# The mixers' input projections in five groups of up to 512 columns, in place of nine of 256

## The chip, the cores and the metric

The kernel runs on one core of one Trainium2 chip. The metric is the device time of one execution in microseconds; lower is better. All times below are of that one core.

## What is computed

The reference is a small language model's forward pass on 256 tokens of width 1024: two layers of a first block, then one layer of another kind with a state-space part and sixteen experts. The change lies in the first block's mixers, of which there is one in each of its two layers:

```python
for l in range(DEPTH):                       # DEPTH = 2
    x = x + 0.5 * swiglu(rmsnorm(x, ffn1_norm[l]), ffn1_wg[l], ffn1_wu[l], ffn1_wd[l])
    h = rmsnorm(x, mix_norm[l]) @ w_in[l]                    # 256 x 1024 @ 1024 x 2290
    h_a, h_b, h_c = jnp.split(h, [A_COLS, A_COLS + B_COLS], axis=-1)
    o_a = mla_mixer(h_a, ...)    # low-rank q and kv, rope, 6 heads of causal attention
    o_b = nsa_mixer(h_b, ...)    # q and kc, vc, ks, vs, kw, vw, gates: compressed, selected, window
    o_c = diff_mixer(h_c, ...)   # q, k, v: 4 heads, the difference of two softmaxes
    x = x + jnp.concatenate([o_a, o_b, o_c], axis=-1) @ w_out[l]
    x = x + 0.5 * swiglu(rmsnorm(x, ffn2_norm[l]), ...)
```

In the second mixer, `kc` and `vc` are compressed: blocks of 32 tokens, 16 apart, plus a position vector, go through `silu(blk @ w1) @ w2`. The second part of the model is untouched by the change.

## The kernel before

Everything is kept in float32 and multiplied in pairs: a weight and an activation are each split into a high half (`h` in `wh`, `xhl`) that is rounded to the matmul's type and a low half (`wl`) with what is left, and a product is the sum of three matmuls, high by high, low by high, high by low. `load` (L145) brings eight chunks of 128 rows by 256 columns into one of four `st` buffers through SP's queue. `split` (L153) makes two `wh` and two `wl` of 1024 columns out of it, in rings of six; ScalarE writes `wh` (L166), VectorE subtracts for `wl` (L167). All matmuls go through `mm` (L97), so their line in the profile is L98, and groups are told apart by their tiles. Plain copies that scale go through a short helper, and stand at L524 in the profile.

A mixer (`_mixer`, L519) has eight banks of PSUM in four rings: `S` three, `T` two, `O` one, `W` two (L313). Its input projection `h` is made in nine groups (L533) of 242 or 256 columns, each for two tiles of 128 tokens, so that a bank `win` of 512 columns holds both. A group has 8 chunks x 2 token tiles x 3 = 48 products. ScalarE then copies its columns out, scaled by the token's inverse norm, into `hA`, `hQ`, `hV`, `hC` and `hW`: `hA` is what the first kind of heads needs, `hQ` and `hV` the second kind's, `hC` and `hW` the third's.

The string `ORDER` (L40) says in which order the steps of a mixer are written: `w` with digits is a group (`w01` two groups in turn), `mp`, `np`, `dp` prepare the three kinds of heads (L626, L770, L886), `m0`, `n0`, `d0` and so on are heads, `df` ends the third kind. A queue of fetches (L573 to L589) is made from the same string: four are issued at the start, and one more behind each group and behind `mp` and `np`. The first groups take the banks `W`, `W`, `S`, `S`, all others the ring `W` (L595).

The order in the text isn't yet the order on the engines. The whole program goes through a scheduler that simulates the engines and orders each one's instructions by its own costs, as far as data and buffers allow.

`np` is the step that matters below. It applies rope to `hQ` (`rtmp`, `hQ`), transposes the columns of `kc` and `vc` (`kvc`, L777, L778), copies them in four pieces to `Z` on ScalarE and VectorE in turn (L784), adds the position vectors (`blk`, L790, four pieces), and multiplies by `phi` (`h<-blk,phi`). The activation of `h` (ScalarE's L797, VectorE's L798) is followed by the small products `kcmp` and `vcmp`. `qtb` and `ktb` are transposes of the second kind's queries and keys; `ks` and `kw` are the keys' copies. `dp` applies rope to `hC`, transposes it (`qct` at L899, `kct` at L900) and copies the keys to `kC` (L905). Then come the scores `S`, the maxima `mx` (L725) and the softmax. At a mixer's end `wo` multiplies by `w_out` (loop at L972).

Of the kernel before, what the change touches and what calls it, by code (L numbers as in the profile page):

```python
# [22 lines left out]
KD = 8  # L23
# [16 lines left out]
ORDER = "w01 w5 w2 mp m0 m1 w8 w3 w4 w6 np w7 dp m2 m3 d0 d1 n0 n1 d2 d3 n2 n3 n4 n5 m4 df m5"  # L40


class Block:
# [128 lines left out]
    def cols(self, w, *segs):  # L172

        wv = w.rearrange("(k p) c -> p k c", p=128)
        out, c = [], 0
        for a, b in segs:
            out.append((c, wv[:, :, a:b]))
            c += b - a
        return self.load(out, wv.shape[1], c)
# [339 lines left out]
    def _mixer(self, l, xops, after):  # L519
# [6 lines left out]
        def tok(name, n, tag=None, bufs=1):  # L526
# [19 lines left out]
        def fetch(i):  # L546
            if i < len(groups):
                units[i] = self.cols(w_in, *groups[i][0])
# [26 lines left out]
        for step in steps:  # L575
            if step[0] == "w":
                for c in step[1:]:
                    queue.append(lambda i=int(c): units.update({i: self.cols(w_in, *groups[i][0])}))
# [18 lines left out]
        def w_in_groups(ids):  # L597

            ws = [self.split(units[i], "k") for i in ids]
            ps = [self.bank(tags.pop(0) if tags else "W", "win") for _ in ids]  # L600
            for k0 in range(KD):
                for k, i, t in ([(k0, i, t) for i in range(len(ids)) for t in range(2)] if len(ids) > 1 else
                                [(k, 0, k0) for k in range(KD)] if k0 < 2 else []):
                    w, p, n = ws[i], ps[i], units[ids[i]][2]
                    o = p[:, t * 256:t * 256 + n]
                    ts = slice(t * 128, (t + 1) * 128)
                    first = t == 0 and k == 0
                    last = t == 1 and k == KD - 1
                    wh, wl = (v[:, k % 4] for v in w[k // 4])
                    self.mm(o, xh[:, k, ts], wh, first, False)  # L610
                    self.mm(o, xh[:, k, ts], wl, False, False)
                    self.mm(o, xl[:, k, ts], wh, False, last)
            for i, p in zip(ids, ps):
                for dst, d, c, m in groups[i][1]:
                    for t in range(2):
                        src = p[:, t * 256 + c:t * 256 + c + m]
                        if isinstance(d, tuple):

                            o = dst[:, t, 0:384].rearrange("p (u c) -> p u c", c=64)[:, d[0] // 64::2][:, 0:d[1]]
                            src = src.rearrange("p (u c) -> p u c", c=64)  # L620
                        else:
                            o = dst[:, t, d:d + m]
                        ACT(o, src, scale=r[:, t:t + 1])
# [329 lines left out]
        for step in steps:  # L953
# [10 lines left out]
            elif step[0] == "w":  # L964
                w_in_groups([int(c) for c in step[1:]])
                for _ in step[1:]:
# [950 lines left out]
```

## Time and profile before

| what | value |
|---|---|
| time, median of three runs | 1533.76 us (1532.36 to 1533.86) |
| time of the profiled execution | 1532.0 us |
| its span in the profile | 1529.8 us |
| busy share of TensorE / VectorE / ScalarE / GpSimd | 98% / 67% / 48% / 6% |
| mixer of the first layer | about 201 to 340 us of the span |
| mixer of the second layer | about 714 to 853 us of the span |

The span runs from the first instruction to the last in the profile; the execution's own time has some 2 us around it. PE is TensorE, DVE VectorE, ACT ScalarE, POOL GpSimd and SP the engine that issues the loads. In a timeline the row of a matmul shows its duration with the pipeline's latency in it, so that what one costs is read from its start to the start of the next. A row that ends in x4 is four instructions in one. The bracket at a row's end is the engine's idle time ahead of it, and the instruction that ended it. The second mixer repeats the first some 512.8 us later.

### The profile page before, as it was taken

Reading aid. Unit: us, or ns where it says so; the run is one execution under the profiler, and the core shown is the slowest. Engines: PE = TensorE matmul, PEld = TensorE weight load, DVE = VectorE, ACT = ScalarE, POOL = GpSimd, SP = SyncE. Lnnn points to the kernel's source line nnn. Section 1 sums busy time; section 2 is a strip of 40 time slices with the busy share of each in tenths; the row PEclk is TensorE's granted clock in tenths of the full one; section 3 lists DMA queues with packets and bytes.
Section 4 is the critical chain, followed back from the end, with each engine's and each line's share of the span. In section 5 each row is a group of like instructions: output and inputs, shape, how many; then the busy total and the mean of one; then the engine's idle time right before and its main releaser. Section 6 shows DMA issues by size and latency. Waiting matters only on the chain.

```text
span 1529.8 us, 25415 instructions
## 1 busy us (share of the span) xinstructions
PE 1492.0 (98%) x9970; PEld 1253.6 (82%) x9970; DVE 1025.1 (67%) x2013; ACT 729.7 (48%) x1382; POOL 91.4 (6%) x142
## 2 busy tenths in 40 slices
PE   8999999999999999999999999999899999999996
PEld 7999998788999989999888999999799987344432
DVE  6886775868677786778576877779988875122112
ACT  6555565755454555455665655547554442011011
POOL 0000000520000000000025000000510100000000
PEclk9999999999999999999999999999999999999999
DMA  7756664216555565655640555566533588999993
GB/s 252 246 175 193 189 164 145 78 56 205 186 188 193 167 193 192 193 192 164 169 130 2 193 185 176 192 192 207 153 123 116 189 296 336 359 393 393 393 394 117
DMA packets 223559, 308.93 MB, mean 202 GB/s; under 512 B 20908, under 2 KB 167608, under 8 KB 223432
## 3 DMA queue, kind: packets, MB, share of 16 engines
q1 hardware_dynamic: 223128, 306.71, 60.1%
q8 instruction: 80, 1.31, 0.4%
q10 hardware_dynamic: 304, 0.53, 0.1%
q14 instruction: 47, 0.39, 0.1%
HBM read 306.16 MB, written 1.05 MB: 201 GB/s over the span
## 4 chain that ended last, share of the span: by engine, by line
PE 92%; DVE 5%; ACT 1%; issue 1%; DMA 0%; POOL 0%; ACTq 0%; DVEq 0%
PE gu L98 32%; PE acc L98 16%; PE proj L98 6%; PE win L98 6%; PE gate L98 4%; PE y L98 4%; PE up L98 4%; PE h L98 3%; PE wo L98 3%; PE S L98 3%; PE moe L98 1%; PE opair L98 1%; PE ptp L691 1%; PE zp L98 1%; PE xgp L98 1%; DVE wl L167 1%
## 5 line engine op out<-in xcount | busy, mean ns | idle before, releaser
L167 DVE TENSOR_TENSOR wl<-st,wh 128x1024 fp32r<-128x1024 f32 (+1 forms) x370 | 447.5, 1220 | 198.9 <-ACT wh L166 187.7
L166 ACT ACTIVATE wh<-st 128x1024 fp32r<-128x1024 f32 (+1 forms) x382 | 399.3, 1059 | 336.5 <-PE gu L98 134.4
L98 PE MATMUL gu<-xhl,wh 128*128 128x512 f32 (+1 forms) x1440 | 487.8, 392 | 3.1 <-ACT wh L166 2.2
L98 PE MATMUL gu<-xhl,wl 128*128 128x256 f32 x1408 | 381.6, 280 | 0.0
L98 PEld LDWEIGHTS gu<-xhl,wh 128*128 128x128 f32 x1440 | 268.2, 190 | 61.0 <-ACT wh L166 2.6
L98 PEld LDWEIGHTS gu<-xhl,wl 128*128 128x128 f32 x1408 | 260.8, 189 | 0.3
L98 PE MATMUL acc<-hx,wh 128*128 128x256 f32 x1408 | 252.1, 281 | 0.0
L98 PEld LDWEIGHTS acc<-hx,wh 128*128 128x128 f32 x1408 | 216.3, 188 | 1.6
L98 PE MATMUL acc<-hx,wl 128*128 128x256 f32 x704 | 196.8, 281 | 0.0
L98 PE MATMUL proj<-uhl,wh 128*128 128x272 f32 (+2 forms) x592 | 127.6, 306 | 5.3 <-DVE dv L1184 1.6
L98 PEld LDWEIGHTS acc<-hx,wl 128*128 128x128 f32 x704 | 132.6, 188 | 0.0
L98 PE MATMUL win<-wh,xhl 128*128 128x256 f32 (+1 forms) x576 | 109.7, 286 | 0.2 <-DVE xT L410 0.2
L98 PEld LDWEIGHTS proj<-uhl,wh 128*128 128x128 f32 x592 | 95.9, 191 | 10.5 <-ACT cv L1222 2.8
L98 PE MATMUL proj<-uhl,wl 128*128 128x272 f32 (+2 forms) x328 | 95.0, 290 | 0.0
L98 PEld LDWEIGHTS win<-wh,xhl 128*128 128x128 f32 x576 | 90.8, 191 | 4.2 <-issue 3.4
L98 PE MATMUL win<-wl,xhl 128*128 128x256 f32 (+1 forms) x288 | 81.9, 284 | 0.0
L394 ACT ACTIVATE hx<-up 128x512 fp32r<-128x512 f32 x44 | 27.7, 630 | 87.8 <-DVE up L393 87.8
L98 PEld LDWEIGHTS proj<-uhl,wl 128*128 128x128 f32 x328 | 62.5, 191 | 0.2
L1814 DVE SCALAR_TENSOR_TENSOR ys<-y,rc,ys 128x512 fp32r<-128x512 f32 x16 | 11.7, 749 | 67.2 <-ACT ys L1634 66.8
L739 POOL TENSOR_SCALAR P<-P,mx 128x128 f32<-128x128 f32 (+2 forms) x88 | 53.2, 621 | 57.9 <-DVE mx L732 41.8
L729 ACT ACTIVATE P<-S,mx 128x256 f32<-128x256 f32 (+2 forms) x128 | 48.9, 394 | 13.4 <-DVE mx L725 3.6
L98 PEld LDWEIGHTS win<-wl,xhl 128*128 128x128 f32 x288 | 55.0, 191 | 0.3
(522 smaller groups left out, 2133.7 us busy)
## 6 DMA issues: line engine op xcount, KB each, us to landing
st<-ffn_wg SPq DMA_DIRECT2D x44, 1024.0 KB, 5.7
st<-ffn_wu SPq DMA_DIRECT2D x44, 1024.0 KB, 5.4
st<-ffn_wd SPq DMA_DIRECT2D x44, 1024.0 KB, 4.7
st<-w_in SPq DMA_DIRECT2D x36, 1024.0 KB, 5.4
st<-w_out SPq DMA_DIRECT2D x16, 1024.0 KB
mf<-expert_w_gate SPq DMA_DIRECT2D x25, 512.0 KB, 9.8
mf<-expert_w_down SPq DMA_DIRECT2D x21, 512.0 KB, 10.7
mf<-expert_w_up SPq DMA_DIRECT2D x18, 512.0 KB, 11.3
```

The lines of the kernel that those rows point to most:

```text
L98: return self.nc.tensor.matmul(out, lhsT, rhs, start=start, stop=stop, skip_group_check=True)
L166: hi = self.nc.scalar.activation(hl[0], src, AF.Copy)
L167: sub = (self.nc.gpsimd if lo[i] == "p" else self.nc.vector).tensor_sub(hl[1], src, hl[0].bitcast(F32))
L394: nc.scalar.activation(hh, up, AF.Copy)
L691: tr(p[:, i * 128:(i + 1) * 128], b, ident)
L729: nc.scalar.activation(P[:, d], s[:, c], AF.Exp, bias=m[:, 0, i:i + 1], accum_out=m[:, 1, i:i + 1])
L739: (nc.gpsimd if key + str(i) in "c0 c1 c2 d0 d1 m0 w0 w1".split() else nc.vector).tensor_scalar(P[:, d], P[:, d], r[:, i:i + 1], None, op0 ...
L1814: V.scalar_tensor_tensor(yl, py[half], rc[:, 1:2], yh.bitcast(F32), op0=OP.mult, op1=OP.subtract)
```

## The change

Four wide groups and one narrow one take the place of the nine. A wide group has up to 512 columns: 498 in the first (`hA` and the last part of `hV`), 512 in the next three. It is loaded in two parts of four chunks by 512 columns, each of which is split in two as before, so loads, bytes and splits per layer stay at 9, the same, and 18. Each product has 512 (498) columns, and the two token tiles have a bank each. The last group `w4` (the second half of `hC`, the third mixer's keys) stays at 256 columns. The banks are `W`, `W` for the first group, `S`, `S` for the second, `W`, `W` for `w2` and `w3`, and one `W` for `w4`. Per layer, 192 wide products and 48 narrow ones stand in the place of 432. The columns are spread over more segments, so the loads of `w_in` are 21 issues a layer on SP's queue where they were 12. The evictions are 22 a layer where they were 24.

```diff
-ORDER = "w01 w5 w2 mp m0 m1 w8 w3 w4 w6 np w7 dp m2 m3 d0 d1 n0 n1 d2 d3 n2 n3 n4 n5 m4 df m5"
+ORDER = "w0 w1 mp m0 m1 w2 w3 np w4 dp m2 m3 d0 d1 n0 n1 d2 d3 n2 n3 n4 n5 m4 df m5"
...
-    def cols(self, w, *segs):
+    def cols(self, w, *segs, part=None):
 
         wv = w.rearrange("(k p) c -> p k c", p=128)
+        if part is not None:
+            wv = wv[:, part * 4:part * 4 + 4]
...
         groups = [
-            ([(0, 256)], [(hA, 0, 0, 256)]),
-            ([(256, 352), (vw0, C0)], [(hA, 256, 0, 96), (hV, 256, 96, 146)]),
-            ([(q0, q0 + 256)], [(hQ, (0, 3), 0, 192), (hQ, 64, 192, 64)]),
-            ([(q0 + 256, vc0)], [(hQ, (192, 2), 0, 128), (hQ, 384, 128, 128)]),
-            ([(ks0, vs0), (kw0, vw0)], [(hQ, 512, 0, 256)]),
-            ([(vc0, ks0), (vs0, kw0)], [(hV, 0, 0, 256)]),
-            ([(C0, C0 + 256)], [(hC, 0, 0, 256)]),
+            ([(0, 352), (vw0, C0)], [(hA, 0, 0, 352), (hV, 256, 352, 146)]),
+            ([(vc0, ks0), (vs0, kw0), (q0, q0 + 256)],
+             [(hV, 0, 0, 256), (hQ, (0, 3), 256, 192), (hQ, 64, 448, 64)]),
+            ([(C0 + 512, C0 + 768), (q0 + 256, vc0)],
+             [(hW, 0, 0, 256), (hQ, (192, 2), 256, 128), (hQ, 384, 384, 128)]),
+            ([(ks0, vs0), (kw0, vw0), (C0, C0 + 256)], [(hQ, 512, 0, 256), (hC, 0, 256, 256)]),
             ([(C0 + 256, C0 + 512)], [(hC, 256, 0, 256)]),
-            ([(C0 + 512, C0 + 768)], [(hW, 0, 0, 256)]),
         ]
...
+        def w_in_group(i):
+
+            w = [piece for u in units[i] for piece in self.split(u, "k")]
+            n = units[i][0][2]
+            wide = n > 256
+            if wide:
+                ps = [self.bank(tags.pop(0) if tags else "W", "win") for _ in range(2)]
+                outs = [p[:, 0:n] for p in ps]
+            else:
+                p = self.bank("W", "win")
+                outs = [p[:, t * 256:t * 256 + n] for t in range(2)]
+            per = KD // len(w)
+            for k in range(KD):
+                wh, wl = (v[:, k % per] for v in w[k // per])
+                for t in range(2):
+                    o, ts = outs[t], slice(t * 128, (t + 1) * 128)
+                    self.mm(o, xh[:, k, ts], wh, k == 0 and (wide or t == 0), False)
                     self.mm(o, xh[:, k, ts], wl, False, False)
+                    self.mm(o, xl[:, k, ts], wh, False, k == KD - 1 and (wide or t == 1))
```

The scheduler's order moves with it. In the first layer, TensorE between the last transposes `kvc` and the step behind `h` reads so before; what is left out ahead of `h` are products of the last group, of which 48 stand between `kvc` and `h` in all:

```order
L98 MATMUL win<-wh,xhl 128x256
L812 MATMUL qtb<-ident,hQ 128x128 x2
L98 MATMUL win<-wh,xhl 128x256
...
L98 MATMUL win<-wh,xhl 128x256
L98 MATMUL h_2952<-blk,phi 128x60 x16
L813 MATMUL ktb<-ident,hQ 128x128
L814 MATMUL ktb<-ident,hQ 128x128
...
L98 MATMUL kcmp<-h_2969,w_2741 64x15 x2
L899 MATMUL qct<-ident,hC 128x128 x4
L98 MATMUL vcmp<-w_2741,h_2969 15x64 x2
L900 MATMUL kct<-ident,hC 128x128 x4
```

And so after, from the last `kvc` on; `h` is in two halves with the transposes `ktb` between them:

```order
L779 MATMUL kvc<-ident,hV 128x128
L813 MATMUL qtb<-ident,hQ 128x128 x2
...
L98 MATMUL win<-wh,xhl 128x256
L813 MATMUL qtb<-ident,hQ 128x128 x2
L98 MATMUL h_2767<-blk,phi 128x60 x8
L814 MATMUL ktb<-ident,hQ 128x128
...
L98 MATMUL h_2767<-blk,phi 128x60 x8
L98 MATMUL kcmp<-h_2784,w_2665 64x15 x2
L900 MATMUL qct<-ident,hC 128x128 x4
L98 MATMUL vcmp<-w_2665,h_2784 15x64 x2
L901 MATMUL kct<-ident,hC 128x128 x4
```

The products that stood between `kvc` and `h` are ten now, with four transposes.

VectorE, from the copies `Z` to the first maximum `mx`, before:

```order
L784 COPY Z<-kvc 64x2x128 x2
L790 TENSOR_TENSOR blk<-Z,v1b 128x8x30 x4
L167 TENSOR_TENSOR wl<-st,wh 128x1024
L513 TENSOR_TENSOR rtmp<-hC,rt 128x16x4
...
L516 TENSOR_TENSOR hC<-hC,rtmp 128x16x8 x2
L167 TENSOR_TENSOR wl<-st,wh 128x1024
L798 SCALAR_TENSOR_TENSOR h_2969<-h_2969,h_2952 64x30
L819 COPY ks<-ktb 64x256
L820 COPY kw<-ktb 64x256
...
L798 SCALAR_TENSOR_TENSOR h_2969<-h_2969,h_2952 64x30
L905 COPY kC<-kct 32x256
L725 TENSOR_REDUCE mx<-S 128x1 x2
```

VectorE after, from the sum of a head (`ohl`) ahead of `Z` on:

```order
L698 TENSOR_TENSOR ohl<-opair,ohl 128x256
L785 COPY Z<-kvc 64x2x128 x2
L515 TENSOR_TENSOR rtmp<-hC,rt 128x16x4
L791 TENSOR_TENSOR blk<-Z,v1b 128x8x30 x4
L516 TENSOR_TENSOR rtmp<-hC,rt 128x16x4
...
L167 TENSOR_TENSOR wl<-st,wh 128x1024
...
L518 TENSOR_TENSOR hC<-hC,rtmp 128x16x8 x2
L820 COPY ks<-ktb 64x256
L821 COPY kw<-ktb 64x256
...
L799 SCALAR_TENSOR_TENSOR h_2784<-h_2784,h_2767 64x30 x2
L906 COPY kC<-kct 32x256 x2
L726 TENSOR_REDUCE mx<-S 128x1 x2
```

The first `rtmp` of `hC` has moved ahead of `blk`, the copies `ks` and `kw` ahead of both steps of `h`, and a second `kC` ahead of the first maximum.

TensorE between the second wide group of the ring `W` (`w2`) and the next (`w3`), after:

```order
L98 MATMUL win<-wl,xhl 128x512
L98 MATMUL win<-wh,xhl 128x512
L98 MATMUL vp<-wm,ckvT 128x384
L98 MATMUL knope<-ckvT,wm 64x256 x4
L98 MATMUL vp<-wm,ckvT 128x384
L98 MATMUL knope<-ckvT,wm 64x256 x2
L98 MATMUL win<-wh,xhl 128x512
```

The low-rank products `vp` and `knope` of the first kind of heads stand between the two groups.

## Rows read from the trace of the kernel before

**Rows 1.** The page's busy times of the engines and the chain's shares by engine.

```profile
PE 1492.0 (98%) x9970; PEld 1253.6 (82%) x9970; DVE 1025.1 (67%) x2013; ACT 729.7 (48%) x1382; POOL 91.4 (6%) x142
PE 92%; DVE 5%; ACT 1%; issue 1%; DMA 0%; POOL 0%; ACTq 0%; DVEq 0%
```

**Rows 2.** Busy times by stretch, both mixers: engines, then granted clock, DMA share, GB/s.

```profile
195.00:330.00 135.00, 132.81 (x1058) 116.85 (x1057) 97.37 (x293) 82.80 (x243) 29.52 (x48) 1.00 0.36 107
715.00:850.00 135.00, 133.03 (x1061) 117.28 (x1060) 95.48 (x293) 83.37 (x243) 28.62 (x47) 1.00 0.34 100
```

**Rows 3.** Chain of waits, first layer's mixer: start, us, engine, tile, line, count.

```profile
202.68 9.64 PE win L98 x81
```

**Rows 4.** TensorE's timeline, products of 256 columns: start, shown us, engine, line, operation.

```profile
215.33 0.40 PE L98 MATMUL win<-wh,xhl 128*128 128x256 f32 x2
...
215.69 0.40 PE L98 MATMUL win<-wh,xhl 128*128 128x256 f32 x2
```

**Rows 5.** TensorE's timeline, products of 512 columns in a later stage.

```profile
1237.34 1.52 PE L98 MATMUL h<-wh,vhl 128*128 128x512 f32 x6
1238.70 0.62 PE L98 MATMUL h<-wl,vhl 128*128 128x512 f32 x2
```

**Rows 6.** Timelines of ScalarE (evictions) and TensorE (`vp`, `knope`).

```profile
246.49 1.14 ACT L524 ACTIVATE hQ<-win,rr 128x128 f32<-128x128 f32 x4 [0.32 <-PE win L98]
...
240.08 0.81 PE L98 MATMUL vp<-wm,ckvT 128*128 128x384 f32 x2
240.82 1.08 PE L98 MATMUL knope<-ckvT,wm 128*64 128x256 f32 x8
```

**Rows 7.** Timeline of all engines, from the last `kvc` to `h`, first layer.

```profile
262.37 0.27 PE L778 MATMUL kvc<-ident,hV 128*128 128x128 f32 x1
...
263.92 0.35 ACT L784 COPY Z<-kvc 64x256 f32<-64x256 f32 x1
264.06 1.22 DVE L167 TENSOR_TENSOR wl<-st,wh 128x1024 fp32r<-128x1024 f32 x1 [0.88 <-ACT wh L166]
...
265.32 0.42 DVE L784 COPY Z<-kvc 64x256 f32<-64x256 f32 x1
...
265.77 0.37 ACT L784 COPY Z<-kvc 64x256 f32<-64x256 f32 x1 [1.00 <-DVE Z L784]
...
266.17 0.43 DVE L784 COPY Z<-kvc 64x256 f32<-64x256 f32 x1 [0.43 <-ACT Z L784]
...
266.63 2.18 DVE L790 TENSOR_TENSOR blk<-Z,v1b 128x240 f32<-128x240 f32 x4
...
268.87 3.67 PE L98 MATMUL h<-blk,phi 128*128 128x60 f32 x32
269.07 0.84 ACT L524 ACTIVATE hC<-win,rr 128x256 f32<-128x256 f32 x2
```

**Rows 8.** The same timeline behind `h`.

```profile
269.86 0.27 DVE L513 TENSOR_TENSOR rtmp<-hC,rt 128x64 f32<-128x64 f32 x1
...
272.58 0.19 ACT L797 ACTIVATE h<-h 64x30 f32<-64x30 f32 x1 [1.73 <-PE h L98]
...
272.84 0.18 DVE L798 SCALAR_TENSOR_TENSOR h<-h,h 64x30 f32<-64x30 f32 x1
...
273.10 0.42 DVE L819 COPY ks<-ktb 64x256 f32<-64x256 f32 x1
...
274.66 0.19 DVE L798 SCALAR_TENSOR_TENSOR h<-h,h 64x30 f32<-64x30 f32 x1
274.90 0.39 PE L98 MATMUL vcmp<-w,h 64*15 64x64 f32 x4 [0.95 <-DVE h L798]
...
276.31 0.42 DVE L905 COPY kC<-kct 32x256 f32<-32x256 f32 x1 [1.47 <-ACT kC L905]
...
276.76 0.62 DVE L725 TENSOR_REDUCE mx<-S 128x1 f32<-128x128 f32 x2
```

**Rows 9.** Chain of waits, the end of the first layer's mixer.

```profile
328.62 13.62 PE wo L98 x112
```

More of the change, by code (lines that the diff above doesn't have):

```diff
@@ L533, in _mixer @@
         groups = [
-            ([(0, 256)], [(hA, 0, 0, 256)]),
-            ([(256, 352), (vw0, C0)], [(hA, 256, 0, 96), (hV, 256, 96, 146)]),
-            ([(q0, q0 + 256)], [(hQ, (0, 3), 0, 192), (hQ, 64, 192, 64)]),
-            ([(q0 + 256, vc0)], [(hQ, (192, 2), 0, 128), (hQ, 384, 128, 128)]),
-            ([(ks0, vs0), (kw0, vw0)], [(hQ, 512, 0, 256)]),
-            ([(vc0, ks0), (vs0, kw0)], [(hV, 0, 0, 256)]),
-            ([(C0, C0 + 256)], [(hC, 0, 0, 256)]),
+            ([(0, 352), (vw0, C0)], [(hA, 0, 0, 352), (hV, 256, 352, 146)]),
[4 more added lines that the diff above has]
+            ([(ks0, vs0), (kw0, vw0), (C0, C0 + 256)], [(hQ, 512, 0, 256), (hC, 0, 256, 256)]),
             ([(C0 + 256, C0 + 512)], [(hC, 256, 0, 256)]),
-            ([(C0 + 512, C0 + 768)], [(hW, 0, 0, 256)]),
         ]
         units = {}
-        def fetch(i):
-            if i < len(groups):
-                units[i] = self.cols(w_in, *groups[i][0])
         small = {}
@@ L576, in _mixer @@
             if step[0] == "w":
-                for c in step[1:]:
-                    queue.append(lambda i=int(c): units.update({i: self.cols(w_in, *groups[i][0])}))
+                i = int(step[1])
+                n = sum(e - b for b, e in groups[i][0])
+                for part in range(2) if n > 256 else [None]:
+                    queue.append(lambda i=i, part=part: units.setdefault(i, []).append(
+                        self.cols(w_in, *groups[i][0], part=part)))
             elif step == "mp":
@@ L595, in _mixer @@
         tags = list("WWSS")
[L597 to L610, printed above, removed]
-                    self.mm(o, xh[:, k, ts], wl, False, False)
[L612 to L623, printed above, removed]
@@ new lines, in w_in_group @@
+        def w_in_group(i):
[14 more added lines that the diff above has]
+                    self.mm(o, xh[:, k, ts], wh, k == 0 and (wide or t == 0), False)
+                    self.mm(o, xh[:, k, ts], wl, False, False)
+                    self.mm(o, xl[:, k, ts], wh, False, k == KD - 1 and (wide or t == 1))
+            for dst, d, c, m in groups[i][1]:
+                for t in range(2):
+                    src = outs[t][:, c:c + m]
+                    if isinstance(d, tuple):
+                        o = dst[:, t, 0:384].rearrange("p (u c) -> p u c", c=64)[:, d[0] // 64::2][:, 0:d[1]]
+                        src = src.rearrange("p (u c) -> p u c", c=64)
+                    else:
+                        o = dst[:, t, d:d + m]
+                    ACT(o, src, scale=r[:, t:t + 1])
@@ L964, in _mixer @@
             elif step[0] == "w":
-                w_in_groups([int(c) for c in step[1:]])
-                for _ in step[1:]:
+                w_in_group(int(step[1]))
+                for _ in units[int(step[1])]:
                     fetch()
```

## Prediction

> **What bounds the kernel now.** I read the page first: TensorE is busy for 98% of the span and the chain of work that ended last lies on it for 92% [rows 1]. Then the two mixers, where the whole change lies: a stretch of 135 us around each has TensorE busy for 132.8 and 133.0 us at full granted clock, with DMA at 0.36 and 0.34 of its share [rows 2]. So in most of a mixer only TensorE's own work counts, and a load or a split that is off its path costs nothing. Then TensorE's timeline, for what a product costs from its start to the next start (its shown duration has the pipeline's latency in it), and last the timeline of all engines between the transposes `kvc` and the first maxima of the heads, because there the chain leaves TensorE and runs over ScalarE and VectorE; what is late in those microseconds is what the change is worth.
>
> **The change part by part.** *Products.* Three products of 256 columns start 0.36 us apart from the next three (215.33 to 215.69), so 120 ns each [rows 4]; in the chain of waits the first 81 of group `w01`, where half have 242 columns, take 9.64 us, 119 ns each [rows 3]. Six products of 512 columns in another part of this kernel, also of fp32r and each with its own weight load, run from 1237.34 to the next start at 1238.70, 227 ns each [rows 5]. The two give (227 - 120) / 256 = 0.42 ns for a column and some 13 ns that a product costs whatever its width. A product of 498 columns is then 221 ns. Per layer 48 products of 498 take the place of 96, and 144 of 512 that of 288: 48 x (238 - 221) + 144 x (240 - 227) = 0.8 + 1.9 = 2.7 us less work on TensorE, 5.4 us for the two layers. The bounds are 0 (a wide product costs two narrow ones) and 2.7 a layer. I take 2.7, since the 512-column rows are the same instruction form.
>
> The trace's fixed cost is 13 ns a product at both widths [rows 4, 5]. The Trainium skill, page "TensorE: Matmul & The Clock Gate", section "Back-to-back issue gap", gives the warm gap as N / 2.4 plus about 2.5 ns, which speaks against this change: an estimate from that page is 192 x 2.5 ns = 0.5 us saved per layer where the rows give 2.7. The trace does not agree with the page's constant.
>
> *Loads, splits, evictions.* Nine loads a layer before, nine after, with the same bytes; the 18 splits a layer keep their 1024 (or 996) columns; ScalarE has 22 evictions instead of 24. The loads are cut into 21 issues instead of 12, all on SP's queue, where DMA stands at a third of its share [rows 2]. I cost these at nothing; the cover is TensorE's queue of products, which lies several microseconds behind the splits.
>
> *Banks.* A group now fills both `W` banks, so the third group's (`w3`) first product must wait for the three evictions of the first bank of `w2`. Four evictions of this kind take 1.14 us [rows 6]. Between the two groups the new order has two `vp` and six `knope`; in the trace one `vp` is a pair of records (240.08 to 240.82, 0.74 us) and four `knope` are eight (1.08), so 2 x 0.74 + 6 x 0.27 = 3.1 us [rows 6]. That covers it. Between `w3` and `w4` stand six `ptp`, some 0.7 us by the pitch of 0.11 that the short products `h` have (3.67 for 32), and the first bank ends three products (0.68 us) before the second; against that stand two evictions of 0.42 (`hC`, 0.84 for two) and 0.3 until a bank can be read [rows 7]: covered by a quarter of a microsecond. Behind the waiting product would stand all of TensorE's queue. I take nothing; uncovered it would be about 1 us a layer.
>
> *What is moved.* The columns of `hQ` come from groups 2, 3, 4 before and are complete with two 256-column groups (6 and 7) still to run. Now they are complete with `w3`, and only `w4` is left. Before, between the last `kvc` (262.37) and the first product `h` (268.87) TensorE had 48 products of group 7, and it did not wait [rows 7]. After, 10 products and four transposes stand there, 10 x 0.12 + 4 x 0.11 + 0.1 for the turn between them = about 1.8 us. What they have to cover is this chain, with the rows of before. The last `kvc` can be read 0.27 after its start. Four copies `Z` run one after the other, ScalarE and VectorE in turn: 0.40 and 0.46 from start to start (265.77 to 266.17, 266.17 to 266.63), 1.7 for the four. Then comes a new wait: VectorE's first `rtmp` of `hC` now stands ahead of `blk`, and it needs ScalarE's first eviction of `w4` (0.42), which follows the second `Z` on ScalarE and the last product of `w4`; with the `rtmp` 0.2. Behind that waiting instruction on VectorE stand `blk`, and behind those TensorE's `h`. Then three `blk` of 0.55 (2.18 for four) [rows 7]. TensorE reaches `h` at 268.87 - 2.7 = 266.2. The last `kvc` is then started at 264.3, the last `Z` ends at 266.3, `hC` is evicted at 266.65, `rtmp` ends at 266.9, the third `blk` at 268.5: TensorE waits 2.3 us that it did not wait before, and `h` starts at 268.5, only 0.4 ahead of before.
>
> *After `h`.* Before, `vcmp` started at 274.90 after 0.95 us of waiting, because four copies `ks`, `kw` (273.10 to 274.66) stood between the two `h` steps on VectorE [rows 8]. Now `ktb` stands in the middle of the `h` products and the copies stand ahead of both `h` steps. VectorE's work from `rtmp` (269.86) to the first `h` step at 272.84, one split in it, took 2.98 us [rows 8]; now 2.8 of it (one `rtmp` is done) follow the fourth `blk` at 269.05: 271.85. The copies, 1.56, end at 273.4; the two `h` steps with the tanh between them take 0.65, to 274.05; TensorE meanwhile does `kcmp` and `qct` (0.7 from 273.6) and starts `vcmp` at 274.3, 0.6 ahead of before. `kct` and the scores follow at that lead.
>
> In the first layer VectorE then has two `kC` copies ahead of the first maximum instead of one, with one of ScalarE's, taken as long, between: 2 x 0.42 = 0.8 more before the maximum that stood at 276.76 [rows 8]. So the first layer comes out 0.2 later than before. In the second layer the order there is as before, and the lead of 0.6 stays. What is late next in both is the softmax, then TensorE, which has the chain again up to the run of `wo` that closes the mixer [rows 9], so I carry the leads to the end.
>
> *Sum:* +0.2 - 0.6 = -0.4 us. The profiled execution took 1532.0 us, which would become 1531.6; the median of the runs shown is 1533.76, 1.8 above it, and becomes **1533.4 us**. Of the 5.4 us that TensorE saves, some 5 are given back at `h` and behind it.
>
> **Rivals.** *The cover is enough* (chance 0.24). If ScalarE and VectorE run further ahead than I walked, or the heads can use what TensorE gained, the full saving stays: 1533.8 - 5.4 = 1528.4 us. For it: the 0.95 us at `vcmp` goes in any case. Against it: TensorE takes its queue in order and has nothing else in front of `h`. From a wait at `h` under about 1 us on, this is the case.
>
> *The products save little* (0.08, slower). The moved chain costs its 2.3 us a layer in any case; only the saving pays for it. With 0.5 us saved a layer, everything up to `h` is 2.2 us later than in the forecast: -0.4 + 2 x 2.2 = +4.0, 1537.8 us. It decides from a saving under 1.0 us a layer on, 5 ns a pair. The six rows at 227 ns speak against it. That is where the Trainium skill's gap, in the section named above, would lead.
>
> *The chain to `h` is longer* (0.14, slower). Each split that stands unfinished ahead of `Z` or `blk` comes on top: before, the first `Z` on VectorE (265.32) stood behind just such a split, `wl` at 264.06, 1.22 us [rows 7]. Now a split of `w_out` stands ahead of `Z` on both queues, and its buffer comes free only at the 24th of the 48 products of `w4`. One late on each engine, ScalarE's taken as long: 2 x (1.22 + 1.22) - 0.4 = +4.5, 1538.2 us. It decides from 1.7 us a layer on. Against it: by my walk that split is over 1 us ahead of `Z`.
>
> **How the numbers follow.** A change of 0.2%, 3.1 us, is about what a measurement of this kernel can tell from none: below 1530.7 is faster, above 1536.8 slower. The forecast and everything near it (a wait of 1 to 4 us at `h`, a bank wait of 1 us) has 0.54, the full saving 0.24, the two slower cases 0.22. The unknown costs of the forecast itself (1 us a layer either way at `h`, up to 1 us a layer at the banks) give 1531 to 1536. The range has to take in the full saving, whose 0.24 alone is more than may be left out, and reaches halfway into the slower cases: 1528.2 to 1537.4.
>
> **What would show it.** Products of 512 columns spaced at 227 ns (right) or 240 (wrong). TensorE idle for about 2.3 us before `h`, released by `blk`, in both layers; no idle there is the first rival. `vcmp` with no wait; `kct` 0.6 us ahead of the same step before, counted from the first product of the mixer; the first maximum no earlier in the first layer. No idle of TensorE ahead of `w3` and `w4` for evictions. I am wrong if the mixers come out more than 1.5 us shorter or longer each.

## The result

The changed kernel takes 1543.34 us in the median of six runs (1543.03 to 1544.51), against 1531.97 us (1529.67 to 1533.86) for the kernel before in six runs. The ratio is 1.0077, with a 95% interval of 1.0067 to 1.0087. The change makes the kernel 11.4 us slower. The prediction was 1533.4 us in a range of 1528.2 to 1537.4, so it was wrong, and on the side to which it gave 0.22. The profiled execution of the changed kernel has a span of 1541.6 us, 11.8 us more than before. The granted clock, as a mean over the span, is 0.984 to 0.986 in all six executions of the changed kernel, and 0.994 in the profiled one before.

Both mixers are longer. From the first product `win` to the first product `gu` of the following stage, by the starts in TensorE's timeline:

| us | before | after | difference |
|---|---|---|---|
| first mixer, first `win` to `h` | 67.28 | 68.89 | +1.61 |
| first mixer, `h` to first `gu` | 73.21 | 78.19 | +4.98 |
| second mixer, first `win` to `h` | 66.78 | 68.43 | +1.65 |
| second mixer, `h` to first `gu` | 73.20 | 79.10 | +5.90 |

That is 14.1 us. Elsewhere the traced execution gains 2.3, of which 1.3 lie ahead of the first mixer, where the traces of all kernels here differ by up to 1.6 us, and 1.3 behind the second.

The first two rows of the page to look at are the busy times, which answer to [rows 1], and the row of the granted clock in 40 slices (tenths of full speed). Each slice is 38.5 us.

```profile
PE 1501.4 (97%) x9586; PEld 1242.1 (81%) x9586; DVE 1023.4 (66%) x2013; ACT 729.0 (47%) x1378; POOL 92.0 (6%) x142
...
PEclk9999999899999999999979999999999999999998
```

TensorE has fewer instructions (9586 for 9970) and is busy for longer. The clock's row has an 8 in the eighth slice and a 7 in the 21st, which are the two mixers; [rows 2] had it at 1.00 there. The stretches of 2 us around `h` in both mixers show it closely: busy time of TensorE, granted clock, DMA share, GB/s.

```profile
266.00:268.00 2.00, 1.07 (x10) 1.00 0.06 15
268.00:270.00 2.00, 0.80 (x7) 1.00 0.02 4
270.00:272.00 2.00, 2.00 (x13) 0.57 0.00 0
272.00:274.00 2.00, 2.00 (x12) 0.50 0.72 175
...
280.00:282.00 2.00, 1.80 (x11) 0.87 0.36 119
...
788.00:790.00 2.00, 1.24 (x7) 0.78 0.00 0
790.00:792.00 2.00, 2.00 (x12) 0.50 0.04 4
...
806.00:808.00 2.00, 2.00 (x16) 0.95 0.00 0
```

In the first mixer TensorE is almost idle from 267 to 269 at a clock of 1.00 and begins `h`; from 270.3 on the clock is 0.50, the lower of its two levels (1.2 GHz for 2.4), until 280.5: 10.2 us. In the second it is at the lower level from 789.1 to 806.2, 17.1 us. TensorE is busy for nearly all of that time, but with instructions that take twice as long. TensorE's timeline there (start, shown us, line, operation, idle time ahead and its releaser):

```profile
266.69 0.38 PE L813 MATMUL qtb<-ident,hQ 128*128 128x128 f32 x2
269.20 2.70 PE L98 MATMUL h<-blk,phi 128*128 128x60 f32 x16 [2.13 <-DVE blk L791]
271.69 0.43 PE L814 MATMUL ktb<-ident,hQ 128*128 128x128 f32 x1
...
272.55 3.51 PE L98 MATMUL h<-blk,phi 128*128 128x60 f32 x16
276.55 0.40 PE L98 MATMUL kcmp<-h,w 64*64 64x15 f32 x4 [0.49 <-DVE h L799]
276.88 1.11 PE L900 MATMUL qct<-ident,hC 128*128 128x128 f32 x4
277.92 0.60 PE L98 MATMUL vcmp<-w,h 64*15 64x64 f32 x4
```

`h` starts 2.5 us after the last `qtb`, and 2.13 of that are a wait for `blk`. Before, it had no wait at all [rows 7]. The first 16 records of `h` begin at the full clock; the second 16 are shown with 3.51 us, nearly what all 32 took before (3.67 [rows 7]). `vcmp`, which waited before [rows 8], no longer waits, but what stands ahead of it takes twice as long.

Ahead of the wait, VectorE and ScalarE do this:

```profile
266.35 0.37 ACT L785 COPY Z<-kvc 64x256 f32<-64x256 f32 x1
...
266.75 0.43 DVE L785 COPY Z<-kvc 64x256 f32<-64x256 f32 x1 [0.47 <-ACT Z L785]
266.88 0.84 ACT L526 ACTIVATE hC<-win,rr 128x256 f32<-128x256 f32 x2 [0.16 <-PE win L98]
...
267.39 0.27 DVE L515 TENSOR_TENSOR rtmp<-hC,rt 128x64 f32<-128x64 f32 x1 [0.21 <-ACT hC L526]
267.58 2.06 DVE L791 TENSOR_TENSOR blk<-Z,v1b 128x240 f32<-128x240 f32 x4
```

This is the chain of the prediction, link by link: the last `Z` on VectorE, then 0.21 us of waiting for ScalarE's eviction of `w4` ahead of `rtmp`, then `blk`.

Last, the price of the products. Three products of 512 columns in a row, and the chain's rows of `qp` ahead of and behind the change (before, then after):

```profile
226.63 0.62 PE L98 MATMUL win<-wh,xhl 128*128 128x512 f32 x2
...
227.31 0.62 PE L98 MATMUL win<-wh,xhl 128*128 128x512 f32 x2
```

```profile
230.44 3.50 PE qp L98 x12
```

```profile
230.88 3.89 PE qp L98 x12
```

Three wide products stand 0.68 us apart, 227 ns each, as [rows 5] had it. But `qp`, products of the first kind of heads that stand between the `win`, cost 0.32 us a record where they cost 0.29. Their order makes them dearer, not the width of what stands beside them. Some have 128 rows and some 64 (the number ahead of the star). The first eight records of that row before, and the first six after (the timeline of a short stretch for each kind, since a longer one merges them):

```profile
230.28 1.13 PE L98 MATMUL qp<-wm,cqT 128*128 128x288 f32 x4
231.34 1.23 PE L98 MATMUL qp<-wm,cqT 64*128 64x288 f32 x4
```

```profile
230.72 0.65 PE L98 MATMUL qp<-wm,cqT 128*128 128x288 f32 x2
231.29 0.75 PE L98 MATMUL qp<-wm,cqT 64*128 64x288 f32 x2
231.97 0.75 PE L98 MATMUL qp<-wm,cqT 128*128 128x288 f32 x2
```

Before, four records of a kind stand in a row here; after, the kind changes with every second one. By the starts in both traces, a record beside a change of kind takes 0.33 to 0.35 us to the next start and any other 0.24, the first one behind a wide product as behind a narrow one. So the first eight records take 2.23 us before and 2.62 after.

Taking the starts of all of TensorE's instructions from the first `win` to `h` in the second mixer, where both kernels have done the same work up to there:

| us, second mixer up to `h` | before | after | difference |
|---|---|---|---|
| 432 or 240 products `win` | 53.14 | 51.07 | -2.07 |
| 16 `qp` | 4.84 | 5.24 | +0.40 |
| 4 records of `vp` | 1.09 | 1.58 | +0.49 |
| 8 records of `opair` | 0.80 | 1.37 | +0.57 |
| 6 `qtb`, with the wait behind the last | 0.49 | 2.84 | +2.35 |
| all else | 6.42 | 6.33 | -0.09 |

The products `win` save 2.07 us, and 1.46 of it is lost on their neighbours. Those stand in another order, which the scheduler made. `qp` was shown above. `opair` had its eight records in one row before, and has them in two now, with products of `w4` between them that are 256 columns wide (first mixer, before and then after):

```profile
259.59 0.87 PE L98 MATMUL opair<-PT,vm 128*64 128x256 f32 x8
```

```profile
261.80 0.65 PE L98 MATMUL opair<-PT,vm 128*64 128x256 f32 x2
...
263.26 0.86 PE L98 MATMUL opair<-PT,vm 128*64 128x256 f32 x6
```

Of the 0.49 at `vp`, 0.39 is what its last record takes, because a `knope` now follows it in place of a `win`; before, that `win` took 0.41 us to the next start, 0.29 more than in a row. Without the wait TensorE is 0.7 us earlier at `h`, not 2.7.

### The profile page after: what moved, and what is told of

Read it like the earlier page. It is cut to its first block, busy times and chain, and to the rows that moved or that the text cites. A ratio compares the mean times of both kernels' runs of the same rounds, so it can differ in the third digit from the quotient of the medians.

```text
span 1541.6 us, 24687 instructions
## 1 busy us (share of the span) xinstructions
PE 1501.4 (97%) x9586; PEld 1242.1 (81%) x9586; DVE 1023.4 (66%) x2013; ACT 729.0 (47%) x1378; POOL 92.0 (6%) x142
## 4 chain that ended last, share of the span: by engine, by line
PE 94%; DVE 4%; ACT 2%; issue 0%; DMA 0%; ACTq 0%; DVEq 0%
PE gu L98 32%; PE acc L98 16%; PE proj L98 7%; PE win L98 7%; PE gate L98 4%; PE h L98 4%; PE y L98 4%; PE up L98 4%; PE wo L98 3%; PE S L98 3%; PE moe L98 1%; PE opair L98 1%; PE zp L98 1%; PE xgp L98 1%; PE ptp L692 1%; PE py L98 1%
## 5 line engine op out<-in xcount | busy, mean ns | idle before, releaser
L167 DVE TENSOR_TENSOR wl<-st,wh 128x1024 fp32r<-128x1024 f32 (+2 forms) x370 | 446.9, 1219 | 204.4 <-ACT wh L166 198.1
L166 ACT ACTIVATE wh<-st 128x1024 fp32r<-128x1024 f32 (+2 forms) x382 | 399.7, 1059 | 335.4 <-PE gu L98 133.7
L98 PE MATMUL win<-wh,xhl 128*128 128x512 f32 (+2 forms) x320 | 94.8, 375 | 0.2 <-DVE xT L412 0.2
L98 PEld LDWEIGHTS win<-wh,xhl 128*128 128x128 f32 x320 | 57.7, 189 | 12.2 <-issue 1.5
L98 PE MATMUL win<-wl,xhl 128*128 128x512 f32 (+2 forms) x160 | 59.7, 373 | 0.0
L167 POOL TENSOR_TENSOR wl<-st,wh 128x1024 fp32r<-128x1024 f32 x12 | 29.1, 2435 | 350.1 <-DVE z L1124 251.4
## 6 DMA issues: line engine op xcount, KB each, us to landing
mf<-expert_w_down SPq DMA_DIRECT2D x21, 512.0 KB, 10.5
```

Of the source, the lines that this page charges most:

```text
L98: return self.nc.tensor.matmul(out, lhsT, rhs, start=start, stop=stop, skip_group_check=True)
L166: hi = self.nc.scalar.activation(hl[0], src, AF.Copy)
L167: sub = (self.nc.gpsimd if lo[i] == "p" else self.nc.vector).tensor_sub(hl[1], src, hl[0].bitcast(F32))
```

## Experiments

Three theories are set against each other. A: the cover behind `kvc` is gone, TensorE waits 2.1 us, and the lowered clock behind the wait makes most of the loss. B: wide products themselves lower the clock, or cost more than they save. C: the order of the heads behind `h` is what costs. In what follows, a mixer's time is from its first `win` to the first `gu`, and the time at half clock is summed over the windows of the trace.

| kernel | median us | ratio to before (95%) | first mixer, us | second mixer, us | at half clock, us |
|---|---|---|---|---|---|
| before | | | 140.49 | 139.98 | 0, 0 |
| changed | 1543.34 | 1.0077 (1.0067 to 1.0087) | 147.08 | 147.53 | 10.2, 17.1 |
| e1_q_early | 1531.98 | 1.0008 (0.9999 to 1.0018) | 144.14 | 140.12 | 10.2, 0 |
| e2_busy | 1536.43 | 1.0028 (1.0018 to 1.0038) | 143.36 | 142.90 | 0, 0 |
| e3_narrow_late | 1555.07 | 1.0164 (1.0149 to 1.0180) | 153.76 | 152.30 | 20.5, 17.1 |
| e4_rope_behind | 1542.39 | 1.0072 (1.0053 to 1.0092) | 146.86 | 145.54 | 13.7, 13.7 |
| e5_q_early_pin | 1538.40 | 1.0056 (1.0044 to 1.0068) | 145.10 | 143.08 | 3.4, 0 |
| e5b_w_last_pin | 1532.07 | 1.0008 (0.9999 to 1.0017) | 141.55 | 141.09 | 0, 0 |
| e6_after_pin | 1542.86 | 1.0078 (1.0063 to 1.0093) | 148.42 | 147.03 | 10.2, 10.2 |
| e7_halves | 1541.68 | 1.0072 (1.0059 to 1.0085) | 148.17 | 145.34 | 17.1, 10.2 |
| e8_busy8 | 1537.06 | 1.0035 (1.0021 to 1.0049) | 143.92 | 145.05 | 6.8, 10.2 |
| e9_w_last_pin36 | 1528.30 | 0.9982 (0.9973 to 0.9991) | 139.69 | 139.25 | 0, 0 |
| e1b_w_last | 1528.86 | 0.9981 (0.9972 to 0.9991) | 141.30 | 139.45 | 3.4, 0 |
| e10_busy8_4 | 1535.72 | 1.0025 (1.0010 to 1.0040) | 143.29 | 142.75 | 0, 0 |

The mixers' columns are those of one profiled execution each. Each ratio is to the kernel before as it was run beside that experiment; its medians there lie between 1530.79 and 1531.97 us.

### The wait and the clock

**e2_busy.** In the changed kernel, ahead of the products `h`:

```diff
             p = self.bank("S", "h1")
+            for j in range(14):
+                self.mm(p[:, 256:384], Z[:, 1], ident, True, True)
             for j in range(16):
```

> The changed kernel with 14 more products ahead of h, of Z by the identity into columns of the bank that nobody reads; they stand on TensorE just where it waits for blk, and nothing else moves but the transposes ktb. Theory A: the wait of 2.1 us is filled by 1.8 us of work (14 x 0.126), the clock stays at 1.0, h starts no later than 0.5 us behind the changed kernel's, and all that the lowered clock cost (some 5 us in the first mixer, 5.9 in the second) comes back although work is added: 1531 to 1535 us. Rival B: 1543 to 1547, clock at half as in the changed kernel. Rival C: the clock at 1.0 but no more than 2 us won, 1541 to 1544.

Measured: 1536.43 us, and both mixers at the full clock. Ten microseconds behind `h` in each mixer (busy, clock, DMA share, GB/s):

```profile
273.00:283.00 10.00, 8.04 (x64) 1.00 0.65 210
789.00:799.00 10.00, 8.04 (x63) 1.00 0.65 211
```

From `h` to the first `gu` it takes 73.11 and 73.09 us, as before the change and 5.1 and 6.0 less than in the changed kernel. Work was added, and the kernel became 6.9 us faster. That speaks for A and against B and C: what was lost behind `h` comes back with the clock, in products of the same width and nearly the same order. The median missed the expected 1531 to 1535: one idle product takes 0.23 us and not 0.126, so that 14 made `h` 1.4 us later than in the changed kernel, in both mixers. The nine times also lie in two groups, four at 1532.7 to 1534.1 and five at 1536.4 to 1537.6 with the traced one among them; what parts them, no run here tells.

**e3_narrow_late.** In the kernel before, only the order of the steps:

```diff
-ORDER = "w01 w5 w2 mp m0 m1 w8 w3 w4 w6 np w7 dp ...
+ORDER = "w01 w5 w2 mp m0 m1 w8 w3 w6 w4 np w7 dp ...
```

> The kernel before with one thing changed in the string of steps: the group that completes hQ (w4) is taken behind w6, as the last but one. Products stay 256 columns wide. No product then stands between the last kvc and h. Theory A: TensorE waits some 3.5 us at h in both layers (chain of 4.2 us from kvc to the third blk, six qtb on top of it), the clock falls to half behind it as in the changed kernel, and each mixer is 8 to 9.5 us longer than before: 1548 to 1552 us. Rival B (only wide products lower the clock): the wait alone, 2 x 3.5 = +7, 1537 to 1540, clock 1.0. Rival C: 1533 to 1540.

Measured: 1555.07 us, beyond what A expected. Waits of TensorE in the first mixer (us in total, times, longest):

```profile
PE h L98 <- DVE blk L790: 3.7, 1, 3.7
PE qtb L812 <- ACT qT L524: 1.7, 1, 1.7
```

And 10 us behind `h` in both mixers, with the clock behind the count:

```profile
275.00:285.00 10.00, 9.33 (x48) 0.50 0.25 84
801.00:811.00 10.00, 9.33 (x48) 0.50 0.23 76
```

Products of 256 columns lose the clock in the same way when what stands behind `kvc` is gone. Here `qtb` waits too, for a copy that frees its bank, which was not foreseen. B falls: the width of the products doesn't decide it.

**e4_rope_behind.** In the changed kernel, VectorE's rope of `hC` behind the fourth `blk`:

```diff
-            for t in range(2):
-                self.rope(hC[:, t] ...
+            with self.behind(small["blk"]):
+                for t in range(2):
+                    self.rope(hC[:, t] ...
```

> The changed kernel with the rope of hC held behind the fourth blk on VectorE, so that blk no longer waits for ScalarE's eviction of w4. Everything else in the same order. By the trace of the changed kernel blk then starts at 267.2 in place of 267.66 (the last Z copy starts at 266.75, 0.43), and the wait at h shrinks from 2.1 to some 1.6 us. Theory A with a fall of the clock only behind the longer wait: clock at 1.0 in one layer or both, 1532 to 1538. Theory A where 1.6 us is still enough for the clock to fall: 2 x 0.5 us less, 1541 to 1543. Rivals B and C: 1542 to 1544.

Measured: 1542.39 us. TensorE's wait at `h` in the first mixer:

```profile
PE h L98 <- DVE blk L791: 1.8, 1, 1.8
```

The wait is 1.8 us in place of 2.1, and the clock falls as in the changed kernel, for 13.7 us in each mixer. The new wait of VectorE for the eviction, which the prediction made much of, is worth 0.3 us a layer; the rest of the wait is the chain itself.

**e8_busy8** and **e10_busy8_4.** e8_busy8 is e2_busy with 8 idle products in place of 14. e10_busy8_4 adds four more behind the last `h`:

```diff
+            for j in range(8):
+                self.mm(p[:, 256:384], Z[:, 1], ident, True, True)
             for j in range(16):
-                self.mm(p[:, 0:60], phi[:, j], ...
+                last = self.mm(p[:, 0:60], phi[:, j], ...
+            with self.behind(last.ins):
+                for j in range(4):
+                    self.mm(p[:, 256:384], Z[:, 1], ident, True, True)
```

> The changed kernel with 8 idle products of Z ahead of h (e2_busy had 14, which took 3.4 us and made h start 1.4 us late). By e2_busy one takes 0.245 us, so 8 take 2.0 and fill the wait without moving h. If the lowered clock is all that the forecast missed: clock 1.0 in both mixers, h at 68.9 and 68.4 us behind the first product as in the changed kernel, from h to the mixer's end 73.1 as before, 2 x 1.4 us less than e2_busy: 1533 to 1534.5, which is the forecast. If the clock falls again: 1541 to 1543.

> e8_busy8, whose clock fell behind a wait of 1.0 us at kcmp right after the 32 short products h, with 4 more idle products of Z (1.0 us) held behind the last h, where that wait was. If the wait there is what lowered the clock in e8_busy8: clock 1.0 in both mixers, kcmp no more than 0.2 us later, from h to the mixer's end 73 to 74 us, each mixer 1 to 2 us behind before: 1533 to 1535, which is the forecast without a fall of the clock. If the clock falls all the same: 1536 to 1538.

e8_busy8 missed: 1537.06 us, with the wait at `h` gone but 6.8 and 10.2 us at half clock. The timeline of TensorE in its first mixer:

```profile
268.30 2.05 PE L98 MATMUL h<-ident,Z 128*128 128x128 f32 x16 [0.17 <-DVE Z L785]
...
270.63 3.68 PE L98 MATMUL h<-blk,phi 128*128 128x60 f32 x32
275.35 0.29 PE L98 MATMUL kcmp<-h,w 64*64 64x15 f32 x4 [1.04 <-DVE h L801]
275.57 0.66 PE L902 MATMUL qct<-ident,hC 128*128 128x128 f32 x4
...
276.55 1.11 PE L903 MATMUL kct<-ident,hC 128*128 128x128 f32 x4
```

The clock falls later here, behind a wait of 1.04 us at `kcmp`: the four transposes `qct` still take 0.66 us, the four `kct` after them 1.11. In the 4.7 us ahead of `kcmp` TensorE did 32 records of 60 columns and nothing else but that wait; before, the like wait of 0.95 came later, at `vcmp` [rows 8], with `ktb`, `kcmp` and `qct` between, and the clock stayed. In e10_busy8_4, where four idle products fill half of the wait at `kcmp` (0.49 us is left), the clock stays in both mixers, and the kernel is again faster with more work: 1535.72 us, though above the 1533 to 1535 that were expected. So here a wait of one microsecond right behind `h` was enough for the clock to fall. Whether the shorter wait or the added work kept it up in e10_busy8_4, the two runs don't part.

### Where the cover comes from

**e1_q_early.** In the changed kernel, the columns dealt out otherwise:

```diff
-            ([(C0 + 512, C0 + 768), (q0 + 256, vc0)],
-             [(hW, 0, 0, 256), (hQ, (192, 2), 256, 128), (hQ, 384, 384, 128)]),
-            ([(ks0, vs0), (kw0, vw0), (C0, C0 + 256)], [(hQ, 512, 0, 256), (hC, 0, 256, 256)]),
+            ([(ks0, vs0), (kw0, vw0), (q0 + 256, vc0)],
+             [(hQ, 512, 0, 256), (hQ, (192, 2), 256, 128), (hQ, 384, 384, 128)]),
+            ([(C0 + 512, C0 + 768), (C0, C0 + 256)], [(hW, 0, 0, 256), (hC, 0, 256, 256)]),
             ([(C0 + 256, C0 + 512)], [(hC, 256, 0, 256)]),
```

> The changed kernel with the columns dealt out otherwise: the third group takes what is left of hQ (ks, kw, the rest of q and kc), the fourth hW and the first half of hC. So hQ is complete one group earlier. TensorE then has 22 products, opair and all six qtb behind the last kvc (some 4 us) where the changed kernel has 10 products and four qtb (1.7 us). Theory A (the 2.1 us wait at h is the cover that went, and the lowered clock behind it is most of the loss): wait at h under 0.5 us, clock 1.0 throughout, each mixer 6 to 7 us shorter than in the changed kernel; 1528 to 1531 us. Rival B (products of 512 columns or what goes with them lower the clock or cost more than they save): stays at 1541 to 1545 with the clock at half behind h. Rival C (the order of the heads behind h is what costs): 1536 to 1543 with the clock at 1.0.

Measured: 1531.98 us. TensorE's waits at `kcmp` and `h` in the first mixer, then in the second, then 10 us behind `h` in each:

```profile
PE kcmp L98 <- DVE h L799: 0.9, 1, 0.9
PE h L98 <- DVE blk L791: 0.8, 1, 0.8
```

```profile
PE kcmp L98 <- DVE h L799: 1.0, 1, 1.0
...
PE h L98 <- DVE blk L791: 0.8, 1, 0.8
```

```profile
270.00:280.00 10.00, 9.04 (x48) 0.67 0.66 210
787.00:797.00 10.00, 8.12 (x62) 1.00 0.67 212
```

With `hQ` complete one group earlier, 11.4 us come back, with the products as wide as in the changed kernel, which again speaks against B. Theory A had 1528 to 1531 with a wait at `h` under 0.5 us and the clock at 1.0 throughout; neither holds. The two mixers have the same waits, and the clock fell in one and not in the other: with waits of 0.8 and 0.9 us this kernel stands at the edge.

**e5_q_early_pin, e5b_w_last_pin, e6_after_pin.** The last group's products are held behind the last `kvc` on TensorE, in e1_q_early, in a third way to deal out the columns, and in the changed kernel:

```diff
-                tr(p[:, 256 + t * 128:384 + t * 128], hV[:, t, 0:128], ident)
+                small["kvc"] = tr(p[:, 256 + t * 128:384 + t * 128], hV[:, t, 0:128], ident).ins
...
-                w_in_group(int(step[1]))
+                with self.behind(small["kvc"]) if step == "w4" else ExitStack():
+                    w_in_group(int(step[1]))
```

e5b_w_last_pin beside it:

```diff
-            ([(C0 + 512, C0 + 768), (C0, C0 + 256)], [(hW, 0, 0, 256), (hC, 0, 256, 256)]),
-            ([(C0 + 256, C0 + 512)], [(hC, 256, 0, 256)]),
+            ([(C0, C0 + 512)], [(hC, 0, 0, 512)]),
+            ([(C0 + 512, C0 + 768)], [(hW, 0, 0, 256)]),
```

> The columns dealt out as in e1_q_early, and the 48 products of the last group held behind the last kvc on TensorE. 40 products, opair and six qtb (some 6.2 us) then stand between kvc and h, and 8 products between h and kcmp. Theory A: no wait at h, none or little at kcmp, clock 1.0 in both mixers, and what is left is the products' own saving, which by the traces of before and after up to h is 0.7 us a layer and not 2.7: 1529 to 1531 us against some 1531 before, each mixer 0.5 to 1.5 us shorter than before. If instead the products save the forecast 2.7 a layer and something else in the changed kernel ate 2 us ahead of h: 1525 to 1527. Rival B (wide products lower the clock): over 1535.

> As e5_q_early_pin, but the fourth group takes the whole of hC and the last one hW, which is needed latest. 41 products between kvc and h, 7 between h and kcmp; hC is complete with the fourth group. Theory A: as e5_q_early_pin within 1 us, with the kC copies and the first maxima no longer behind an eviction of the last group: 1528.5 to 1531.

> The changed kernel, columns as they are, with only the 48 products of the last group held behind the last kvc. 43 products then stand between kvc and h. Theory A: no wait at h, but hQ is complete only at the end of the fourth group, so that TensorE waits for its eviction and rope ahead of kvc instead: 3 to 4 us a layer, with the clock lower behind it; 1540 to 1550. If the rope is done in time (wait under 1 us): 1530 to 1533, and the place of the last group alone was the fault.

Measured: 1538.40, 1532.07 and 1542.86 us, the first two above what they were expected to take. None waits at `h` any more. In e5_q_early_pin and e6_after_pin the wait has moved: `hC` is now complete so late that `qct` waits for its rope. The wait that e6_after_pin was expected to have ahead of `kvc` isn't there. Waits of TensorE in e5_q_early_pin and e5b_w_last_pin, first mixer; e6_after_pin has 1.3 us at `qct` too, and 1.1 at `vcmp`:

```profile
PE qct L900 <- DVE hC L518: 1.3, 1, 1.3
PE vcmp L98 <- DVE h L799: 0.7, 1, 0.7
```

```profile
PE opair L98 <- DVE PT L763: 0.8, 1, 0.8
```

e5b_w_last_pin, with `hC` complete a group earlier, has no wait at `qct`, and the clock is 1.00 in both mixers. Of theory C so much is true: the order costs something by itself. In the second mixer of e5_q_early_pin, at the full clock, it takes 4.1 us more from `h` on than before: 1.0 for the eight products that now stand there, and waits of 1.3 at `qct`, 1.0 at a first `S` for `kC`, and 1.0 at an `S` 45 us behind `h`, none of which before has. That is why its 1538.40 lies where B was expected, and not for B's reason. e5b_w_last_pin is 1.1 us longer than before in each mixer although the products save 0.7: `opair` waits 0.8 us, because VectorE's copy `PT` comes behind part of the rope of `hC`, and an `S` 43 us behind `h` waits 1.0 us that it does not wait before.

**e9_w_last_pin36** and **e1b_w_last.** e5b_w_last_pin with only 36 of the 48 products held, and with none held:

```diff
+                    with self.behind(small["kvc"]) if not wide and k >= 2 else ExitStack():
-                    self.mm(o, xh[:, k, ts], wh, ...
+                        self.mm(o, xh[:, k, ts], wh, ...
```

> e5b_w_last_pin with the first 12 products of the last group free and 36 held behind the last kvc. All 36 then stand ahead of h, none behind it. The wait of opair for PT (0.8 us), which the early kvc brought, should go or halve, TensorE still without a wait at h (16 + 13 + 7 products, opair and six qtb, 5.6 us against a chain of 4 us): 1 us a layer less than e5b_w_last_pin, 1529 to 1531, clock 1.0. Against before 0 to 2 us faster, which is at the limit of what can be told. If a wait at h of over 1 us comes back, the clock falls: 1536 or more.

> e5b_w_last_pin with nothing held: the scheduler puts 22 products behind the last kvc, as in e1_q_early, where TensorE waited 0.8 us at h and 0.9 at kcmp and the clock fell in one of the two mixers. If the first maxima gain by hC being complete a group earlier: 1529 to 1531 with the clock at 1.0, 1532 to 1535 with a fall in one or both.

Measured: 1528.30 and 1528.86 us, both just below their forecasts and 0.2% faster than the kernel before, though in e1b_w_last TensorE still waits 0.6 us at `h` and the profiled execution has 3.4 us at half clock in one mixer. For e9_w_last_pin36, 135 us around each mixer:

```profile
195.00:330.00 135.00, 132.84 (x872) 1.00 0.35 106
707.00:842.00 135.00, 133.03 (x875) 1.00 0.35 105
```

`h` starts 66.49 and 66.04 us behind the first `win`, 0.8 and 0.7 earlier than before, from `h` on it takes 73.20 and 73.21 us, as before, and each mixer is 0.8 and 0.7 us shorter. So the regrouping is worth 0.7 to 0.8 us a layer when nothing waits for what it moved. The two mixers make 1.5 of the 2.7 us by which the median lies below before's; the traces show what the rest may be (before has 10 us at half clock between 1100 and 1300 us, this execution none), but no run here tells why.

### The price of the width

**e7_halves.** e5_q_early_pin with each wide product cut in two:

```diff
-                    self.mm(o, xh[:, k, ts], wh, ...
+                    for a in (0, 256) if wide else (0,):
+                        b = min(a + 256, n)
+                        oo, hh, ll = o[:, a:b], wh[:, a:b], wl[:, a:b]
+                        self.mm(oo, xh[:, k, ts], hh, ...
```

> e5_q_early_pin with each wide product cut in two of 256 (or 242) columns, from the same loads and splits into the same banks. Tells what a wide product saves by itself. By the pitch of products in a row (227 against 2 x 120 ns, 224 against 234) it should be 2.3 us a layer slower than e5_q_early_pin, 4.7 in all; by what the whole stretch up to h showed, 0.7 a layer, 1.4 in all. So 1530.5 to 1532 or 1534 to 1536. Clock 1.0 in both mixers.

Inconclusive as a time: 1541.68 us. The scheduler put all 48 products of the last group ahead of `h` and TensorE waited 1.4 us there; the clock fell. Its wait at `h` in the first mixer:

```profile
PE h L98 <- DVE blk L794: 1.4, 1, 1.4
```

Up to `h` it still answers. In the second mixer `h` comes at 68.55, less the wait 67.15; e5_q_early_pin has it at 65.82, with 8 products (0.96) fewer ahead of it and a wait of 0.6 at `opair`, so 66.2. So e7_halves is about 1.0 us a layer slower up to `h`, near the 0.7 and far from the 2.3 of the pitch. But the width is not all that differs. `qp`, `vp` and `opair` cost in e7_halves no more than before the change (4.84, 0.70 and 0.80 us in the second mixer, for 5.24, 1.58 and 1.37 in e5_q_early_pin), and they stand much as before again: `qp` with four records of a kind in a row, `opair` in one row, a `win` behind both pairs of `vp`. Taken together, `win` and `vp` take 54.51 us in e7_halves, less the wait, and 52.26 in e5_q_early_pin with the eight products added. That is 2.25 for the width, near the 2.3 of the pitch; `qp`, `opair` and `ptp` in their other order give 1.3 of it back. The dearer neighbours come with the order that the scheduler makes around wide products. No run here keeps that order fixed and changes the width alone.

## Why the prediction was wrong

*Products.* The pitch was nearly right: 120 and 227 ns, and 224 for 498 columns where 221 was worked out; products of 242 columns stand 114 ns apart where the sum has 118. That makes 2.35 us a layer and not 2.7. The term as a whole measured 0.7. `win` saved 2.07, and `qp`, `vp` and `opair` gave back 1.46: the scheduler put them in another order, and the sum has no term for that. This step failed too, by 2.0 us a layer. It meets the condition of the rival "The products save little" (under 1.0 us a layer, chance 0.08); with 0.7 in place of 2.7 the forecast becomes 1537.4. The Trainium skill's constant (page "TensorE: Matmul & The Clock Gate", section "Back-to-back issue gap") would have come to 0.5, near the truth, but not by its own reason: the trace has 13 ns a product beyond the columns' time, as the prediction said, and the saving was lost on other instructions.

*Loads, splits, evictions, banks.* Right. TensorE waits for none of them; the only wait of a `win` product is 0.19 us at the start, for `xT`, which was there before.

*The wait at `h`.* Right in place, cause and size: 2.3 us forecast, 2.13 measured in both mixers, released by `blk`, with `rtmp` waiting for the eviction ahead of it. But `h` starts 1.6 us later than before and not 0.4 earlier: the 2.0 us between are the missing part of the products' saving.

*After `h`.* This is the step that failed most. The prediction had +0.6 us behind `h` in the first mixer and -0.2 in the second; +5.0 and +5.9 were measured, 10.5 of the 14.5 us by which its mixers miss. The lead of 0.6 us at `vcmp` was worked out with durations at the full clock, and so were the maxima and the heads behind. [rows 2] had the clock at 1.00, and the prediction took that for a property of the stretch; it asked what a wait of 2.3 us costs and answered 2.3 us. In the trace 5 to 6 us more are lost, because the clock falls behind it: where e2_busy fills the wait, the clock stays and they are not lost. No rival had this. "The chain to `h` is longer" came to 1538.2 by more wait, not by the clock. The Trainium skill, same page, section "Part 1: The HAM clock gate", states that the clock has two levels and that a TensorE that was idle is put back to the lower one. The trace agrees: 0.50 behind the wait. That a wait of 2.1 us is enough for it, the trace alone tells. It was not weighed as a rival. With the measured 5.0 and 5.9 us behind `h` in place of its own terms the forecast of -0.4 would have been +10.1, and with 0.7 for the products as well +14.1, which is what the two mixers show. The execution as a whole is 11.8 longer, because 2.3 were gained elsewhere.

*Chances.* 0.54 went to a forecast that priced a wait at its own length. That the bound "1 to 4 us of wait at `h`" was put down as harmless to the result is the same error once more.

## What to carry to other kernels

Where TensorE sets the time, a wait that a change opens on it is not priced by its length alone: look at the granted clock behind waits of the same length elsewhere, and take the work that follows at half speed as a case of its own. A product's pitch in an undisturbed row told here what the rows of products save (2.35 us a layer), and not what the stretch saves (0.7): the small products between the rows were put in another order, and that has to be priced too, from the new order on the engine. And what a regrouping makes complete last mattered more here than how well its products run: dealing the same columns to five groups in another way, so that the next chain's inputs come early, took 14.5 us off the changed kernel (e1b_w_last).

## What the runs showed of the hardware

- Behind a wait of 2.1 us the clock was at its lower level for 10.2 us in one mixer and 17.1 in the other, with TensorE 95% and 97% busy in that time. Behind waits of 0.8 and 0.9 us, with 32 records of 60 columns and four transposes between them, it fell in one mixer of e1_q_early and not in the other, and so it did behind waits of 0.6 and 0.5 us in e1b_w_last. In e8_busy8 a wait of 1.0 us right behind those 32 records was enough in both, while waits of 0.92 to 0.99 us some steps later (before, e9_w_last_pin36) left it at 1.00. The length of the wait alone does not tell in these runs whether the clock falls.
- Idle work in the place of a wait made the kernel faster: 14 products that nobody reads took 6.9 us off.
- Products `qp` of 288 columns, some of 128 rows and some of 64, take 0.24 us a record from start to start among their like, and 0.33 to 0.35 beside a change from one number of rows to the other: the same eight records took 2.23 us in one order and 2.62 in another.
